# Recurrent mixer of a two-block network: small products ordered over the quarters of the matmul array, two PSUM banks at a time

## The chip, the cores and the metric

The kernel runs on one core of a Trainium2 chip. Its time is the time of one execution on the device, in microseconds (us). TensorE (PE) multiplies matrices into PSUM; VectorE (DVE), ScalarE (ACT) and GpSimd (POOL) do the rest; SyncE (SP) issues most of the transfers.

## The reference, cut to what matters

A sequence of 256 tokens of width 1024 goes through a first block of two layers (a mixer of three branches, then a feed-forward part) and a second block (an attention layer and a state-space layer, with a second, "context", sequence beside). All arithmetic is float32. The change touches one branch of the first block's mixer, the recurrence over tokens, in both directions, of eight heads of 64 channels:

```python
def step(state, inp):
    r_t, w_t, k_t, v_t, kk_t, a_t = inp
    sa = jnp.einsum('bhij,bhj->bhi', state, -kk_t)
    state = (state * w_t[:, :, None, :] + sa[..., None] * (kk_t * a_t)[:, :, None, :]
             + v_t[..., None] * k_t[:, :, None, :])
    return state, jnp.einsum('bhij,bhj->bhi', state, r_t)
...
y = direction(0, False) + direction(1, True)
```

## The kernel before, in words

Large products use weights that are split on the chip into a rounded high part (ACT, line 57) and the rest (DVE or POOL, line 58), and are made of three matmuls each (lines 185 to 187). Weights come from DRAM by SP's queue (line 172) into a ring of four buffers.

The recurrence is turned into small products over four chunks of 64 tokens. `wkv_groups` runs four groups per layer, each of two heads `h`, two directions `d` and four chunks (tile of 128 tokens `t`, half of it `q`), so eight groups in all. A 64-row and 64-column product sits on one quarter of the 128 by 128 array: the half of the partitions of its operands chooses the rows, the half of the partitions of its output the columns. `hs(0)` and `hs(1)` are these halves. A float32 product shows in the trace as two matmul instructions, each with its weight load.

`wkv_group` is a Python generator. It goes beside the large products: each call of `up` (a large product of 24 matmuls) ends with `tick`, which takes the next steps of the generators beside it (2.4 steps per call in layer 0, 1.6 in layer 1, `RATES`). A step is what stands between two `yield`s. The framework then lays out the instructions of each engine in a fixed order: it takes, among those whose inputs are ready in its own model of the times, the one that was emitted first. So a step whose inputs are late is mixed with large products, and on the chip each engine follows the fixed order. What is left of the generator is emitted by `drain("wk")` before the third branch is merged.

The group's steps that the change touches:

- line 585, `ps_l`: matrices between the tokens of a chunk, for `LR` and `AK`. For each head one PSUM bank and one step: eight products, `q` innermost, so two quarters alternate (the rows are those of the head). DVE masks the bank (line 587).
- lines 718, 719 and 721, `ps_n`: what each chunk adds to the state. One bank for each of two halves `b` of the work; three products of one quarter stand together (two only for the first chunk), then those of the other head. Half `b` uses the rows of `q = b`.
- line 735, `ps_c`: the corrections of the states at the chunks' ends, the second (`s = 2`) after the first (`s = 1`), in one step; one small bank for each direction, two products each, read by two instructions of DVE (line 737).
- line 748, `ps_q`: for each `q` a bank with eight products, the columns alternating with the head; DVE adds to it in two instructions (line 750).
- line 769, `ps_y`: the outputs, 30 products of a group in one bank: for each `t` and `q` first one or two with all 128 rows (64 columns, states), then six on the quarter of rows `q` and columns `q`.

All these take turns in three PSUM banks (tag `pa`). Line 691 (`ps_ak`) and line 701 are not touched; they alternate the quarters of rows and columns `q`, within one bank:

```python
for u, (d, h, t) in enumerate(ui):
    for q in range(2):
        mm(pak[hs(q), u], AK8[hs(q), u, 0:64], Vt[hs(q), t, hs(h)], start=True, stop=True)
```

Of the kernel before, what the change touches and what calls it, by code (L numbers as in the profile page):

```python
# [14 lines left out]
P = 128  # L15
# [10 lines left out]
# 2 atanh(z) / z in powers of z^2, |z| <= 1/3  # L26
# [10 lines left out]
# constants of the first block  # L37
# [10 lines left out]
class Weights:  # L48
    """a tile of weights as pairs of rounded high and low parts, made in two pieces."""
# [18 lines left out]
class Core:  # L68
    NR, NH = 4, 5
    dom = "sm"  # L70
    # pairs whose low parts are left to GpSimd, where VectorE has a chain to finish
# [92 lines left out]
    def wsplit(self, src, a, b, rows=False):  # L164
        """a tile [128, a, b] of weights as a pair; src may be two halves, of the last dimension or, with rows, of the partitions."""
# [39 lines left out]
    def fill(self, first=()):  # L205
        """emits work that doesn't depend on x, for the tensor engine to do while the rows of x are normalized; the weights `first` that x meets are loaded before."""
# [17 lines left out]
    def tick(self):  # L224
        """emits the next steps of the work that goes beside."""
# [24 lines left out]
    def drain(self, name=None):  # L250
        """emits the rest of the work beside."""
# [13 lines left out]
    def rsqrt(self, x, n, out=None):  # L265
        """x [128, n] -> x ** -0.5 by Newton's method."""
# [12 lines left out]
    def rsqrt1(self, x):  # L279
        """x [128, 1] -> x ** -0.5 by Newton's method."""  # L280
# [10 lines left out]
    def evac_T(self, src, gcol, bcol, dst, ps=None):  # L291
        """src [128 tok, 2, 128*n] token-major -> dst pair [128, n, 256], channel c scaled and shifted."""
# [13 lines left out]
        for j in range(0, n, 2):  # L306
# [6 lines left out]
            # one engine reads a bank  # L313
# [16 lines left out]
    def ln_rows(self, v, t, rows=None, eps=1e-5):  # L330
        """v[:, t] normalized in place; with rows of scales and shifts, these too."""
# [16 lines left out]
    def layernorm(self, v, gcol, bcol):  # L348
        """v [128 tok, 2, 1024], normalized already; returns the pair of x^T."""
# [9 lines left out]
    def padded(self, tiles):  # L359
        """tiles with zeros in the first and the last column."""  # L360
# [5 lines left out]
    def scaled(self, v, grow, brow, scale):  # L366
        """v [128 tok, 2, 1024], normalized already, becomes scale * x."""
# [7 lines left out]
    def row(self, ap, name="row", q=None):  # L375
        """a vector [n] of DRAM on every partition."""
# [6 lines left out]
class First(Core):  # L383
# [27 lines left out]
    def derived(self, l):  # L411
        """per-channel constants of the layer that are worked out on the chip."""
# [24 lines left out]
    def toeplitz(self):  # L437
        """relb[p, h, c] = rel_bias[bucket(c - p - 128), h], c in 0..383."""
# [17 lines left out]
    def shift(self, l, zt, dst):  # L456
        """project tile zt of the shifted part of w_in and apply the centred token shift; dst [128, 256]."""
# [33 lines left out]
    def wkv_group(self, l, ct):  # L491
        """heads 2 ct and 2 ct + 1, both directions; the result takes the place of r."""
# [84 lines left out]
        for dst, src in ((LR, Bn), (AK, K)):  # L577
            for h in range(2):
                yield
                pl = self.pa([P, 2, 2, P], "ps_l")  # L580
                for d in range(2):
                    for t in range(2):
                        for q in range(2):
                            c = 2 * t + q
                            mm(pl[hs(q), d, t], src[hs(h), d, c * 64:(c + 1) * 64],
                               AR[hs(h), :, d, c * 64:(c + 1) * 64], start=True, stop=True)
                v_.tensor_tensor(dst[:, :, h], pl, self.m_lr.unsqueeze(2).to_broadcast([P, 2, 2, P]), op=ALU.mult)
        # v meets the sum of both directions
# [4 lines left out]
        # blocks of 8 on the diagonal by substitution, each matrix spread over the partitions of its block's rows  # L593
# [23 lines left out]
        # X[:, 1] is the inverse, X[:, 0] its transpose as long as it is of blocks up to 32  # L617
# [26 lines left out]
        # the blocks of 32 off the diagonal, A U B; both directions' share tiles  # L644
# [64 lines left out]
        dcol = lambda d, s: Dt[:, d * 4 + (s if d == 0 else 2 - s):d * 4 + (s if d == 0 else 2 - s) + 1]  # L709
        for b in range(2):  # L710
            pn = self.pa([P, 3, 2, 64], "ps_n")
            for s in range(3):
                d = (s + b) % 2
                c = chunk(d, s)
                t, q = divmod(c, 2)
                for h in range(2):
                    u = d * 4 + h * 2 + t
                    mm(pn[hs(h), s, 0], Bt[hs(q), d, t, hs(h)], WU(hs(q), u, slice(64, 128)), start=True, stop=False)
                    mm(pn[hs(h), s, 0], Kt[hs(q), d, t, hs(h)], Vt[hs(q), t, hs(h)], start=False, stop=True)
                    if s:  # L720
                        mm(pn[hs(h), s, 1], WU(hs(q), u, slice(0, 64)), Bt[hs(q), d, t, hs(h)], start=True, stop=True)
# [9 lines left out]
        for s in (1, 2):  # L731
            for d in range(2):
                pc = self.pa([P, 64], "ps_c")
                for h in range(2):
                    mm(pc[hs(h)], MT[hs(h), d, s - 1], S0[hs(h), d, s - 1, hs(h)], start=True, stop=True)
                for h in range(2):
                    v_.scalar_tensor_tensor(S0[hs(h), d, s, hs(h)], pc[hs(h)], dcol(d, s)[hs(h)], N0[hs(h), d, s - 1],
                                            op0=ALU.mult, op1=ALU.add)
        yield
        Q = self.w1("xx", [P, 2, 2, 2, 64], bufs=self.NX)  # L740
        Rt = AR[:, 1].rearrange("p d (t q i) -> p q d t i", q=2, i=64)
        for q in range(2):
            pq = self.pa([P, 2, 2, 64], "ps_q")
            for d in range(2):
                for t in range(2):
                    for h in range(2):
                        u = d * 4 + h * 2 + t
                        mm(pq[hs(h), d, t], WU(hs(q), u, slice(0, 64)), LR8[hs(q), u, 64:128], start=True, stop=True)
            for d in range(2):
                v_.tensor_tensor(Q[:, q, d], pq[:, d], Rt[:, q, d], op=ALU.add)  # L750

        yield
        py = self.pa([P, 2, P], "ps_y")
        for t in range(2):
            for q in range(2):
                o = py[hs(q), t]
                seq = []
                for d in range(2):
                    c = 2 * t + q
                    s = c if d == 0 else 3 - c  # L760
                    if s:
                        seq.append((o, Q[:, q, d, t], S0[:, d, s - 1]))
                for h in range(2):
                    for d in range(2):
                        u = d * 4 + h * 2 + t
                        seq.append((o[:, hs(h)], LR8[hs(q), u, 64:128], WU(hs(q), u, slice(64, 128))))
                    seq.append((o[:, hs(h)], AK8[hs(q), h * 2 + t, 64:128], Vt[hs(q), t, hs(h)]))
                for i, (oo, a, b) in enumerate(seq):
                    mm(oo, a, b, start=(i == 0), stop=(i == len(seq) - 1), skip_group_check=True)
# [30 lines left out]
    def pool_branch(self, l, j, ya):  # L800
        """groups j and j + 1 of the pooling branch, in two steps."""
# [42 lines left out]
    def down(self, acc, w, k0, nk, x, first, last):  # L844
        """acc[t][h] [128 tok, 512] += x[:, k0..]^T w rows; w [K, 1024] in DRAM, x pair [128, nk, 256]."""
# [109 lines left out]
    def branch(self, l, n, y, m):  # L955
        """m [128, 8, 256] (+)= (1 + tanh(gate / 2)) * (y @ w_branch[n])."""
# [24 lines left out]
    def resid(self, acc, ax, scale, rows=None):  # L981
        """the normalized rows of scale * acc + ax."""
# [8 lines left out]
    def layer(self, l, ax, rows):  # L991
        """ax: the normalized rows, still without the scales and shifts in DRAM."""
# [78 lines left out]
    def start(self):  # L1071
        """x, and what its norm needs, before all else."""
# [25 lines left out]
class Second(Core):  # L1098
    """the second block. The context and the modulation vectors don't depend on x; what they need is emitted beside the first block."""
# [74 lines left out]
    def upto(self, n):  # L1174
        """the same in steps."""
# [4 lines left out]
    def need(self, n):  # L1180
        """emits what is left of the first n parts of the modulation vectors."""
# [3 lines left out]
    def rms(self, x, t):  # L1185
        """[128, 1]: the rows' 1 / sqrt(mean square + eps) of x[:, t]."""
# [10 lines left out]
    def modulate(self, x, l, row, which, dst, *first, inplace=False, ps=None):  # L1197
        """dst pair = the modulated rmsnorm of x, transposed; which 0 for the mixer, 1 for the ffn."""
# [15 lines left out]
    def add_gated(self, x, t, h, g, acc):  # L1214
        """x[:, t, half h] += g * acc."""
# [5 lines left out]
    def down2(self, wtile, kb, pair, res, gate):  # L1221
        """res += gate * (pair^T w); wtile(k, n, h): k tiles k..k+n-1 of w, half h of its columns."""
# [17 lines left out]
    def ffn_ahead(self):  # L1240
        """the first hidden tiles of the context's ffn, to DRAM."""
# [7 lines left out]
    def swiglu1(self, l, j, x):  # L1249
        """the products for hidden tile j of the ffn."""  # L1250
# [715 lines left out]
def _consts():  # L1966
    """arrays that depend on the shapes alone."""
    import numpy as np
    k = {}
# [124 lines left out]
```

## Time and profile before

| | |
|---|---|
| median of 3 runs | 2550.89 us (2545.45 to 2552.18) |
| profiled execution, span from first to last instruction | 2544.6 us |
| TensorE busy | 2403.8 us, 94% |
| VectorE busy | 1810.9 us, 71% |
| ScalarE busy | 1238.4 us, 49% |
| GpSimd busy | 391.8 us, 15% |
| mean traffic of the DMA engines | 159 GB/s |

The profile page gives the profiled execution by its span alone; the runs' times are 0.9 to 7.6 us above it. Busy time is the union of an engine's instructions. Matmuls are pipelined, so the duration of one (0.22 us for a 64 by 64 one) is no cost: the cost is the distance from its start to the start of the next.

### The profile page before, as it was taken

Reading aid. Unit: us, or ns where it says so; the run is one execution under the profiler, and the core shown is the slowest. Engines: PE = TensorE matmul, PEld = TensorE weight load, DVE = VectorE, ACT = ScalarE, POOL = GpSimd, SP = SyncE. Lnnn points to the kernel's source line nnn. Section 1 sums busy time; section 2 is a strip of 40 time slices with the busy share of each in tenths; the row PEclk is TensorE's granted clock in tenths of the full one; section 3 lists DMA queues with packets and bytes.
Section 4 is the critical chain, followed back from the end, with each engine's and each line's share of the span. In section 5 each row is a group of like instructions: output and inputs, shape, how many; then the busy total and the mean of one; then the engine's idle time right before and its main releaser. Section 6 shows DMA issues by size and latency. Waiting matters only on the chain.

```text
span 2544.6 us, 49580 instructions
## 1 busy us (share of the span) xinstructions
PE 2403.8 (94%) x19082; PEld 2104.7 (83%) x19082; DVE 1810.9 (71%) x3997; ACT 1238.4 (49%) x2615; POOL 391.8 (15%) x376
## 2 busy tenths in 40 slices
PE   7999999999998999999999999899899989989998
PEld 5777777788997888778988899778799889987997
DVE  7757866677667858777778666866666689985666
ACT  3334425555553444243455455555555556654554
POOL 4200210122003100200012200300200233231000
PEclk9999999999999999999999999999999989999999
DMA  8744446456666644465556566512466644436664
GB/s 243 234 128 146 139 140 131 141 173 186 184 199 193 186 149 123 124 206 151 166 149 195 171 186 199 131 35 71 145 185 186 174 118 129 125 104 198 209 184 132
DMA packets 513005, 404.94 MB, mean 159 GB/s; under 512 B 49968, under 2 KB 445024, under 8 KB 512000
## 3 DMA queue, kind: packets, MB, share of 16 engines
q1 hardware_dynamic: 511536, 397.41, 52.9%
q0 software_dynamic: 1232, 4.36, 0.5%
q8 instruction: 150, 2.46, 0.4%
q14 instruction: 87, 0.71, 0.1%
HBM read 393.19 MB, written 8.52 MB: 158 GB/s over the span
## 4 chain that ended last, share of the span: by engine, by line
PE 72%; DVE 15%; DMA 4%; ACT 4%; issue 3%; POOL 1%; SPq 0%; ACTq 0%; DVEq 0%; POOLq 0%
PE ps_fg L185 5%; PE ps_fg L186 5%; PE ps_fg L187 4%; PE ps_acc L186 4%; PE ps_acc L187 4%; PE ps_acc L185 4%; DVE wl L58 3%; DMA wr<-in_w_in_dram 2%; PE ps_up L187 2%; PE ps_up L186 2%; PE ps_up L185 2%; PE ps_o L1452 2%; PE acc L185 2%; PE acc L186 2%; PE acc L187 2%
## 5 line engine op out<-in xcount | busy, mean ns | idle before, releaser
L57 ACT CAST wh<-wr 128x512 fp32r<-128x512 f32 (+1 forms) x1212 | 743.7, 622 | 839.7 <-PE ps_fg L186 169.3
L58 DVE TENSOR_TENSOR wl<-wr,wh 128x512 fp32r<-128x512 f32 x1092 | 774.2, 717 | 410.2 <-ACT wh L57 403.3
L58 POOL TENSOR_TENSOR wl<-wr,wh 128x512 fp32r<-128x512 f32 (+1 forms) x120 | 159.8, 1351 | 825.6 <-ACT wh L57 816.6
L186 PE MATMUL ps_fg<-xl,wh 128*128 128x256 f32 x672 | 190.2, 283 | 0.0
L187 PE MATMUL ps_fg<-xh,wl 128*128 128x256 f32 x672 | 190.2, 283 | 0.0
L185 PE MATMUL ps_fg<-xh,wh 128*128 128x256 f32 x672 | 190.1, 283 | 0.0
L186 PE MATMUL ps_acc<-wl,hh 128*128 128x512 f32 x432 | 171.9, 398 | 8.9 <-DVE wl L58 8.9
L185 PE MATMUL ps_acc<-wh,hh 128*128 128x512 f32 x432 | 171.0, 396 | 0.0
L187 PE MATMUL ps_acc<-wh,hl 128*128 128x512 f32 x432 | 170.9, 396 | 0.0
L187 PE MATMUL ps_up<-xh,wl 128*128 128x256 f32 x480 | 135.9, 283 | 0.4 <-POOL wl L58 0.4
L185 PE MATMUL ps_up<-xh,wh 128*128 128x256 f32 x480 | 135.8, 283 | 0.0
L186 PE MATMUL ps_up<-xl,wh 128*128 128x256 f32 x480 | 135.8, 283 | 0.0
L185 PEld LDWEIGHTS ps_fg<-xh,wh 128*128 128x128 f32 x672 | 129.0, 192 | 0.4
L186 PEld LDWEIGHTS ps_fg<-xl,wh 128*128 128x128 f32 x672 | 129.0, 192 | 0.4
L187 PEld LDWEIGHTS ps_fg<-xh,wl 128*128 128x128 f32 x672 | 129.0, 192 | 0.0
L186 PEld LDWEIGHTS ps_acc<-wl,hh 128*128 128x128 f32 x432 | 81.9, 190 | 28.6 <-DVE wl L58 11.1
L185 PE MATMUL ps_fg<-ch,wh 128*128 128x256 f32 x352 | 102.9, 292 | 0.0
L186 PE MATMUL ps_fg<-cl,wh 128*128 128x256 f32 x352 | 101.1, 287 | 0.0
L187 PE MATMUL ps_fg<-ch,wl 128*128 128x256 f32 x352 | 100.3, 285 | 0.8 <-DVE wl L58 0.8
L185 PE MATMUL ps_gl<-xh,wh 128*128 128x256 f32 x336 | 98.8, 294 | 0.1
L187 PEld LDWEIGHTS ps_acc<-wh,hl 128*128 128x128 f32 x432 | 81.9, 190 | 19.1 <-DVE hl L263 0.2
L185 PEld LDWEIGHTS ps_acc<-wh,hh 128*128 128x128 f32 x432 | 81.9, 190 | 18.0 <-ACT hh L262 0.2
(656 smaller groups left out, 6865.7 us busy)
## 6 DMA issues: line engine op xcount, KB each, us to landing
wr<-in_w_in_dram SPq DMA_DIRECT2D x110, 512.0 KB
adw<-in_ada_w_dram SPq DMA_DIRECT2D x96, 512.0 KB
wr<-in_ssm_w_in_dram SPq DMA_DIRECT2D x72, 512.0 KB
wr<-in_ffn_w_gate_dram SPq DMA_DIRECT2D x66, 512.0 KB
wr<-in_ffn_w_up_dram SPq DMA_DIRECT2D x66, 512.0 KB
wr<-in_ffn_w_down_dram SPq DMA_DIRECT2D x66, 512.0 KB
wr<-in_w_up_dram SPq DMA_DIRECT2D x64, 512.0 KB
wr<-in_w_down_dram SPq DMA_DIRECT2D x64, 512.0 KB
```

Of the source, the lines that this page charges most:

```text
L57: nc.scalar.copy(hi, raw[:, i:i + self.n])
L58: z = (nc.gpsimd if core.spare > 0 else nc.vector).tensor_tensor(lo, raw[:, i:i + self.n], hi.bitcast(F32), op=ALU.subtract)
L185: mm(out, ah, bh, start=first, stop=False)
L186: mm(out, ah, bl, start=False, stop=False)
L187: mm(out, al, bh, start=False, stop=last)
L1452: mm(po[HS[e], c, t], kvs[kb // 2][1][:, kb % 2, g * 64:(g + 1) * 64], at[:, kb], start=(kb == 0), stop=(kb == nk - 1))
```

## The change

The same products are computed, with the same operands. Their order and their banks change, and so do the steps. The rest of the diff takes out comments and docstrings.

```diff
         for dst, src in ((LR, Bn), (AK, K)):
-            for h in range(2):
-                yield
-                pl = self.pa([P, 2, 2, P], "ps_l")
-                for d in range(2):
-                    for t in range(2):
+            yield
+            pls = [self.pa([P, 2, 2, P], "ps_l") for _ in range(2)]
+            for d in range(2):
+                for t in range(2):
+                    for h in range(2):
                         for q in range(2):
                             c = 2 * t + q
-                            mm(pl[hs(q), d, t], ...
+                            mm(pls[h][hs(q), d, t], ...
-                v_.tensor_tensor(dst[:, :, h], pl, ...
+            for h in range(2):
+                v_.tensor_tensor(dst[:, :, h], pls[h], ...
+            yield
...
+        pns = [self.pa([P, 3, 2, 64], "ps_n") for _ in range(2)]
+        for s in range(3):
+            for i in range(3 if s else 2):
+                for b in range(2):
+                    pn = pns[b]
+                    d = (s + b) % 2
+                    t, q = divmod(chunk(d, s), 2)
+                    for h in range(2):
+                        (the product i of the three, as before)
         for b in range(2):
-            pn = self.pa([P, 3, 2, 64], "ps_n")
-            (for each s and h: the two or three products)
+            pn = pns[b]
...
-        for s in (1, 2):
-            for d in range(2):
-                pc = self.pa([P, 64], "ps_c")
-                for h in range(2):
-                    mm(pc[hs(h)], MT[hs(h), d, s - 1], S0[hs(h), d, s - 1, hs(h)], start=True, stop=True)
-                (two instructions of DVE)
-        yield
+        def step(s):
+            pc = self.pa([P, 2, 64], "ps_c")
+            for d in range(2):
+                for h in range(2):
+                    mm(pc[hs(h), d], MT[hs(h), d, s - 1], S0[hs(h), d, s - 1, hs(h)], start=True, stop=True)
+            (four instructions of DVE)
+        step(1)
+        yield
+        step(2)
+        yield
...
-        for q in range(2):
-            pq = self.pa([P, 2, 2, 64], "ps_q")
-            for d in range(2):
-                for t in range(2):
+        pqs = [self.pa([P, 2, 2, 64], "ps_q") for _ in range(2)]
+        for d in range(2):
+            for t in range(2):
+                for q in range(2):
                     for h in range(2):
                         u = d * 4 + h * 2 + t
-                        mm(pq[hs(h), d, t], ...
+                        mm(pqs[q][hs(h), d, t], ...
-            for d in range(2):
-                v_.tensor_tensor(Q[:, q, d], pq[:, d], Rt[:, q, d], op=ALU.add)
+        for q in range(2):
+            v_.tensor_tensor(Q[:, q], pqs[q], Rt[:, q], op=ALU.add)
...
         py = self.pa([P, 2, P], "ps_y")
+        seq = [[], []]
...
+        (seq[q]: first the products with states, of both t; then the others, t outermost)
-                for i, (oo, a, b) in enumerate(seq):
-                    mm(oo, a, b, start=(i == 0), stop=(i == len(seq) - 1), skip_group_check=True)
+        for i in range(len(seq[0])):
+            for q in range(2):
+                mm(*seq[q][i], start=(i == 0), stop=(i == len(seq[q]) - 1), skip_group_check=True)
```

A group has one step more than before (the correction's second half is a step of its own); the steps around `ps_l` keep their number. Each half of `seq` has 15 products, three of them with 128 rows.

## Rows read from the trace of the kernel before

**Rows 1.** The page: the chain that ended last, by engine.

```profile
PE 72%; DVE 15%; DMA 4%; ACT 4%; issue 3%; POOL 1%; SPq 0%; ACTq 0%; DVEq 0%; POOLq 0%
```

**Rows 2.** Busy time by stretch: stretch, length, then each engine, clock, DMA.

```profile
100.00:390.00 290.00, 278.29 (x3354) 225.54 (x3353) 216.28 (x672) 109.06 (x248) 47.30 (x61) 0.99 0.49 147
390.00:500.00 110.00, 108.22 (x699) 85.21 (x699) 66.73 (x190) 61.82 (x177) 4.44 (x4) 1.00 0.52 128
500.00:850.00 350.00, 328.28 (x2209) 298.54 (x2208) 243.08 (x403) 173.88 (x311) 71.35 (x51) 0.97 0.63 188
850.00:1235.00 385.00, 372.79 (x3952) 312.75 (x3952) 287.38 (x796) 150.89 (x323) 34.35 (x49) 0.99 0.50 151
```

**Rows 3.** Busy time on ps_y, ps_l, ps_n and ps_c, then L748 by line.

```profile
sum 850.00, PE 42.55 PEld 34.27 DVE 6.77; mean PE 21.27 PEld 17.14 DVE 3.38
...
sum 850.00, PE 28.78 PEld 23.51 DVE 21.48; mean PE 14.39 PEld 11.76 DVE 10.74
...
sum 850.00, PE 20.15 PEld 17.85 DVE 20.13; mean PE 10.07 PEld 8.93 DVE 10.06
...
sum 850.00, PE 12.38 PEld 7.59 DVE 18.13; mean PE 6.19 PEld 3.79 DVE 9.06
...
L748 PE MATMUL ps_q<-w_LR,w_xx 64*64 64x64 f32 x256 | 8.4, 224 | 0.0
```

**Rows 4.** Timeline of PE at a group's outputs: start, us, instruction, count.

```profile
381.41 0.43 PE L769 MATMUL ps_y<-s,w_xx 128*64 128x128 f32 x2 [0.45 <-DVE w_xx L750]
381.77 0.44 PE L769 MATMUL ps_y<-w_xx,w_LR 64*64 64x64 f32 x4
...
382.61 0.65 PE L769 MATMUL ps_y<-s,w_xx 128*64 128x128 f32 x4
383.19 0.44 PE L769 MATMUL ps_y<-w_xx,w_LR 64*64 64x64 f32 x4
```

**Rows 5.** Timeline of PE at L691, and what comes next.

```profile
140.39 1.15 PE L691 MATMUL ps_ak<-w_Vt,w_AK 64*64 64x64 f32 x32
141.47 0.39 PE L187 MATMUL ps_qk<-xh,wl 128*128 128x256 f32 x1
```

**Rows 6.** Timeline of PE at L585: one head, then two heads mixed.

```profile
187.73 1.09 PE L585 MATMUL ps_l<-w_AR,w_Bn 64*64 64x128 f32 x16
188.75 1.13 PE L906 MATMUL ps_lg<-ak,aq 64*128 64x256 f32 x4
...
192.60 0.28 PE L585 MATMUL ps_l<-w_AR,w_Bn 64*64 64x128 f32 x2
192.66 0.28 PE L585 MATMUL ps_l<-w_AR,w_K 64*64 64x128 f32 x2
192.71 0.28 PE L585 MATMUL ps_l<-w_AR,w_Bn 64*64 64x128 f32 x2
```

**Rows 7.** Timeline of PE at ps_n.

```profile
146.83 0.22 PE L718 MATMUL ps_n<-w_xx,w_Bt 64*64 64x64 f32 x1
146.83 0.22 PE L721 MATMUL ps_n<-w_Bt,w_xx 64*64 64x64 f32 x1
146.84 0.22 PE L718 MATMUL ps_n<-w_xx,w_Bt 64*64 64x64 f32 x1
146.88 0.22 PE L719 MATMUL ps_n<-w_Vt,w_Kt 64*64 64x64 f32 x1
```

**Rows 8.** Timeline of PE at the corrections, two groups.

```profile
149.38 0.28 PE L187 MATMUL ps_qk<-xh,wl 128*128 128x256 f32 x1
149.50 0.28 PE L185 MATMUL ps_qk<-xh,wh 128*128 128x256 f32 x1
149.71 0.45 PE L735 MATMUL ps_c<-s,w_MT 64*64 64x64 f32 x8
...
233.89 0.32 PE L735 MATMUL ps_c<-s,w_MT 64*64 64x64 f32 x2
```

**Rows 9.** Timeline of DVE at the corrections.

```profile
150.48 1.23 DVE L737 SCALAR_TENSOR_TENSOR s<-ps_c,Dt,w_N 64x64 f32<-64x64 f32 x4
```

More of the change, by code (lines that the diff above doesn't have):

```diff
@@ L577, in wkv_group @@
         for dst, src in ((LR, Bn), (AK, K)):
-            for h in range(2):
-                yield
-                pl = self.pa([P, 2, 2, P], "ps_l")
-                for d in range(2):
-                    for t in range(2):
+            yield
[3 more added lines that the diff above has]
+                    for h in range(2):
                         for q in range(2):
                             c = 2 * t + q
-                            mm(pl[hs(q), d, t], src[hs(h), d, c * 64:(c + 1) * 64],
+                            mm(pls[h][hs(q), d, t], src[hs(h), d, c * 64:(c + 1) * 64],
                                AR[hs(h), :, d, c * 64:(c + 1) * 64], start=True, stop=True)
-                v_.tensor_tensor(dst[:, :, h], pl, self.m_lr.unsqueeze(2).to_broadcast([P, 2, 2, P]), op=ALU.mult)
+            for h in range(2):
+                v_.tensor_tensor(dst[:, :, h], pls[h], self.m_lr.unsqueeze(2).to_broadcast([P, 2, 2, P]), op=ALU.mult)
+            yield
         g_.tensor_tensor(AK[:, 0, :, :, 64:128], AK[:, 0, :, :, 64:128], AK[:, 1, :, :, 64:128], op=ALU.add)
@@ L709, in wkv_group @@
         dcol = lambda d, s: Dt[:, d * 4 + (s if d == 0 else 2 - s):d * 4 + (s if d == 0 else 2 - s) + 1]
-        for b in range(2):
-            pn = self.pa([P, 3, 2, 64], "ps_n")
[L712 to L715, printed above, removed]
-                for h in range(2):
[L717 to L721, printed above, removed]
+        pns = [self.pa([P, 3, 2, 64], "ps_n") for _ in range(2)]
[6 more added lines that the diff above has]
+                    for h in range(2):
+                        u = d * 4 + h * 2 + t
+                        if i == 0:
+                            mm(pn[hs(h), s, 0], Bt[hs(q), d, t, hs(h)], WU(hs(q), u, slice(64, 128)), start=True, stop=False)
+                        elif i == 1:
+                            mm(pn[hs(h), s, 0], Kt[hs(q), d, t, hs(h)], Vt[hs(q), t, hs(h)], start=False, stop=True)
+                        else:
+                            mm(pn[hs(h), s, 1], WU(hs(q), u, slice(0, 64)), Bt[hs(q), d, t, hs(h)], start=True, stop=True)
+        for b in range(2):
+            pn = pns[b]
             for s in range(3):
@@ L730, in wkv_group @@
         yield
-        for s in (1, 2):
-            for d in range(2):
-                pc = self.pa([P, 64], "ps_c")
-                for h in range(2):
-                    mm(pc[hs(h)], MT[hs(h), d, s - 1], S0[hs(h), d, s - 1, hs(h)], start=True, stop=True)
-                for h in range(2):
-                    v_.scalar_tensor_tensor(S0[hs(h), d, s, hs(h)], pc[hs(h)], dcol(d, s)[hs(h)], N0[hs(h), d, s - 1],
-                                            op0=ALU.mult, op1=ALU.add)
-        yield
         Q = self.w1("xx", [P, 2, 2, 2, 64], bufs=self.NX)
         Rt = AR[:, 1].rearrange("p d (t q i) -> p q d t i", q=2, i=64)
-        for q in range(2):
-            pq = self.pa([P, 2, 2, 64], "ps_q")
+        def step(s):
+            pc = self.pa([P, 2, 64], "ps_c")
             for d in range(2):
-                for t in range(2):
+                for h in range(2):
+                    mm(pc[hs(h), d], MT[hs(h), d, s - 1], S0[hs(h), d, s - 1, hs(h)], start=True, stop=True)
+            for d in range(2):
+                for h in range(2):
+                    v_.scalar_tensor_tensor(S0[hs(h), d, s, hs(h)], pc[hs(h), d], dcol(d, s)[hs(h)], N0[hs(h), d, s - 1],
+                                            op0=ALU.mult, op1=ALU.add)
+        step(1)
[6 more added lines that the diff above has]
+                for q in range(2):
                     for h in range(2):
                         u = d * 4 + h * 2 + t
-                        mm(pq[hs(h), d, t], WU(hs(q), u, slice(0, 64)), LR8[hs(q), u, 64:128], start=True, stop=True)
-            for d in range(2):
-                v_.tensor_tensor(Q[:, q, d], pq[:, d], Rt[:, q, d], op=ALU.add)
+                        mm(pqs[q][hs(h), d, t], WU(hs(q), u, slice(0, 64)), LR8[hs(q), u, 64:128], start=True, stop=True)
+        for q in range(2):
+            v_.tensor_tensor(Q[:, q], pqs[q], Rt[:, q], op=ALU.add)
         yield
         py = self.pa([P, 2, P], "ps_y")
+        seq = [[], []]
         for t in range(2):
             for q in range(2):
-                o = py[hs(q), t]
-                seq = []
                 for d in range(2):
@@ L761, in wkv_group @@
                     if s:
-                        seq.append((o, Q[:, q, d, t], S0[:, d, s - 1]))
-                for h in range(2):
+                        seq[q].append((py[hs(q), t], Q[:, q, d, t], S0[:, d, s - 1]))
+        for t in range(2):
+            for h in range(2):
+                for q in range(2):
+                    o = py[hs(q), t, hs(h)]
                     for d in range(2):
                         u = d * 4 + h * 2 + t
-                        seq.append((o[:, hs(h)], LR8[hs(q), u, 64:128], WU(hs(q), u, slice(64, 128))))
-                    seq.append((o[:, hs(h)], AK8[hs(q), h * 2 + t, 64:128], Vt[hs(q), t, hs(h)]))
-                for i, (oo, a, b) in enumerate(seq):
-                    mm(oo, a, b, start=(i == 0), stop=(i == len(seq) - 1), skip_group_check=True)
+                        seq[q].append((o, LR8[hs(q), u, 64:128], WU(hs(q), u, slice(64, 128))))
+                    seq[q].append((o, AK8[hs(q), h * 2 + t, 64:128], Vt[hs(q), t, hs(h)]))
+        for i in range(len(seq[0])):
+            for q in range(2):
+                mm(*seq[q][i], start=(i == 0), stop=(i == len(seq[q]) - 1), skip_group_check=True)
         yield
```

## Prediction, made before the changed kernel ran

> **What bounds the kernel now.** I read the page first. Its chain of waits runs 72% through TensorE and 15% through VectorE [rows 1], so TensorE's time counts, but not all of it. Then the stretches. The recurrent mixer's small products stand in two: in 100 to 390 us TensorE is busy 278.3 of 290 us, in 850 to 1235 us 372.8 of 385 us, at a granted clock of 0.99 [rows 2], its 2.4 GHz level. TensorE is full there, 96 and 97%; VectorE is at 75% in both (216.3 of 290, 287.4 of 385). After the first, 390 to 500 us is dense too, 108.2 of 110 us [rows 2]: the mixer's chain has ended there and other products go on. So no one waits for the mixer's last step; what is taken from TensorE inside the stretch moves all that follows. Only then the small products themselves, by tile and by timeline.
>
> The reader is to see one thing in the timelines: the cost of a small matmul is the distance between starts, and this depends on its neighbours. In the outputs (`ps_y`) twelve matmuls of one quarter stand between 381.77 and 382.61 us [rows 4]: 0.84 us, 0.07 each with the changes of shape. Where two quarters alternate, 32 of the same shape take 140.39 to 141.47 us [rows 5]: 1.08 us, 0.034 each. So two quarters overlap, and the stretch costs half. In `ps_l` 16 matmuls of 64x128 on two quarters of one head take 187.73 to 188.75 us, 1.02 us for 8 pairs, 0.13 a pair; where the end of one head's work meets the start of the other's, pairs start at 192.60, 192.66 and 192.71 us, 0.055 apart [rows 6]. That is four quarters at once: the second pair of quarters, other rows and another bank, costs nothing. In `ps_n` four matmuls of 64x64 start within 146.83 to 146.88 us [rows 7], so these overlap beyond two as well.
>
> **The change part by part.** The measure is busy time on TensorE over both stretches [rows 3], eight groups.
>
> Outputs, `ps_y`: 42.55 us, 5.3 a group. A group has 12 matmuls with 128 rows and 48 on quarters. Two of the former take 0.36 us with the change of shape (381.41 to 381.77), four 0.58 (382.61 to 383.19) [rows 4]: 0.11 each and 0.14 for the change. Afterwards they stand together and their column halves alternate: 6 pairs by 0.11 and 0.14 once are 0.80 us. The 48 alternate as in rows 5: 1.08 us for 32 and 16 more by 0.03 (0.06 a pair) are 1.56. Together 2.36 against 5.3: 2.9 a group, 23 us. Bounds: if the 128-row halves do not overlap, which no row shows for this shape, 6 x 0.11 x 8 = 5 less, 18; if the quarters do not (48 by 0.058, which is 0.84 less 0.14 over twelve, and 0.22 at the edges, 3.0), 3.8 a group, 12 saved; if neither does, 4.5, and only the fewer changes of shape are left: 6 us. I take 23, since rows 5 are the same shape and the same alternation.
>
> Chunk matrices, `ps_l`: 28.78 us. Afterwards 16 bursts (two per group) of 32 matmuls on four quarters. By rows 6 a burst of eight fours costs what eight pairs cost now, 1.09 us with its tail: 17.4. Saved: 11 us. Bounds: 0 if the second pair is not free, 11 if it is; rows 6 show it, so I take 11.
>
> State parts, `ps_n`: 20.15 us, 2.5 a group. 64 matmuls in 16 fours; at 0.058 a four, the distance of pairs in rows 5, 0.93, and 0.22 at the edges (1.15 less 16 x 0.058 in rows 5), 1.2 us. But the half `b = 1` needs the other direction's copy from ScalarE, so I expect the burst to fall in two, the first on two quarters only: 1.6. Saved: 0.9 a group, 7 us. Bounds: with pairs only 32 by 0.058 and the edges twice, 2.3, saves 2; one full burst 10. I take 7.
>
> Corrections, `ps_c`: 12.38 us. In the first correction eight stand together, 0.45 us; the second falls into bursts of two, 0.32 each [rows 8]. An entry costs also the matmul before it 0.09 (149.50 to 149.71 is 0.21, the usual distance, 149.38 to 149.50, 0.12). Both whole would be 16 x 0.45 = 7.2 and three entries less per group, 2: 7 us saved. The second still waits for each of VectorE's four instructions, so it may stay split and save nothing. I take 4, nearly the middle: in a step of its own more of the four is done by then.
>
> State products, `ps_q`: 8.4 us. 16 pairs by 0.06 become 8 fours, 0.48 less in each group if the fours overlap wholly; with the edges I take 3 us, bounds 0 and 4. VectorE's additions fall from 32 instructions to 16, which is off the path.
>
> One step more per group delays the mixer's end by a call of `up` or two per layer. That is hidden by the dense stretch behind [rows 2]; without it, some 3 us a call. No weight, DMA or issue is moved. VectorE's two masks of a pair of heads now come after both, off the path for the same reason.
>
> Sum: 23 + 11 + 7 + 4 + 3 = 48 us of TensorE; by the lower bounds 6 + 0 + 2 + 0 + 0 = 8, by the upper 23 + 11 + 10 + 7 + 4 = 55. How much arrives? At most the 96 to 97% of a full TensorE, at least the chain's 72%. Weights must come some 7% faster (48 of 675 us): 147 and 151 GB/s become about 160, and 500 to 850 us runs at 188 [rows 2], so the supply holds. I take 80%, nearer to the chain, for its part on VectorE does not shrink: 38 us. The profiled span, 2544.6 us, becomes 2506; it lies 6.3 us under the median, so the time is 2550.9 - 38, 2512 to 2513. I say 2512.
>
> A rule speaks against the largest term. In the outputs the alternating quarters lie in different rows but write one bank. Rows 5 have just that and show 0.034 us each. The Trainium skill, TensorEngine Tiling (Array Packing), section Gotcha 1: PSUM Pressure, says that different row tiles cannot use the same PSUM bank at the same time. By it the outputs would save 12 us, as in the second bound above, and the sum would be 37; by the trace 23 and 48. The trace decides for this shape.
>
> A second one touches the fours of 64 columns. Rows 7 show four starts in 0.05 us. The Trainium skill, TensorE: Matmul & The Clock Gate, section "Wait — 56ns, not 53.3ns?", gives a floor of about 25 ns between starts, by which a four would cost an estimated 0.1 us, `ps_q` would save nothing and `ps_n` 3, and the sum would be 41. The rows show less between starts, so I keep 48.
>
> **The rivals.**
>
> Pairs only (15%). Row halves exclude each other where the order is steady, and rows 6 and 7 show only seams between two pieces of work. Then `ps_l` and `ps_q` save nothing, `ps_n` 2, the corrections 4; the outputs keep 23 if one bank is no obstacle, 12 if it is. 29 or 18 us, by 80% 23 or 14: 2528 to 2537. For it: no long run on four quarters is in the trace. Against: rows 6, three pair starts at half the distance. It is also what the first rule above would bring.
>
> Supply takes half (12%). TensorE gets ahead of the splits of weights: VectorE, 75% busy, does them between the mixer's own instructions, and the wait moves to the large products. Half of 48 arrives: 2527. Against: VectorE has a quarter free.
>
> All of it arrives (13%), since VectorE no longer stands at the front of its queue behind `ps_y` for 5.3 us: 48 to 55 us, 2496 to 2503.
>
> Slower (5%). The three banks: two are taken at once, so TensorE, whose order is fixed, stands where the next pair of banks, or the second correction with all four states in one bank, waits for VectorE; four of its instructions take 1.23 us [rows 9]. If it stood that long at six places of a group (both `ps_l`, `ps_n`, both corrections, `ps_q`), this is 6 x 8 x 1.23 = 59 us against 48: 11 us slower, 2562. It decides from 1.0 us a place on. Behind it are large products, and all engines that wait for them. Against: TensorE now has only 11.7 and 12.2 us free in the two stretches [rows 2], with the same three banks.
>
> That the products do not change place, since the framework reorders them, is the case of no change (5%): it mixes only what is not ready, and within a step all becomes ready together.
>
> **How the numbers follow.** Forecast 50%, its own range 2503 to 2526. Low end 2490: all 55 us and 5 of waits. High end 2540: a little over the worse end of "pairs only"; "slower", "no change" and a little more are left out, about 12%. Over 0.3% is 7.7 us, 2543 and 2559 the marks, about what can be told from no change here. Faster: 50 + 15 + 12 + 13, less 2 for tails: 88%. Same: 5 and these 2, 7%. Slower 5%.
>
> **What would show it.** `ps_y` near 2.4 us a group as one burst, the 128-row matmuls first; `ps_l` as 16 bursts of about 1.1 us; busy time on `ps_l` near 17, `ps_n` 13, `ps_y` 19. Wrong if a burst of four quarters takes twice 1.1 us, if `ps_y` stays at 0.058 a matmul, or if TensorE's free time in the two stretches grows by more than 20 us.

## The result, and the profile after

The changed kernel takes 2512.68 us, the median of four runs (2510.18 to 2514.42), against 2548.17 us of the kernel before beside it: ratio 0.9868, 95% interval 0.9851 to 0.9884, 35.5 us less. The forecast was 2512. In a later round its ratio was 0.9869 (0.9847 to 0.9892).

The page of the profiled run (2511.67 us, span 2509.7): busy time by engine, and further down the chain that ended last, which answers to [rows 1].

```profile
PE 2359.1 (94%) x19082; PEld 2072.0 (83%) x19082; DVE 1811.0 (72%) x3981; ACT 1234.1 (49%) x2615; POOL 388.9 (15%) x376
...
PE 70%; DVE 16%; DMA 5%; issue 4%; ACT 4%; POOL 1%; SPq 0%; DVEq 0%; ACTq 0%; POOLq 0%
```

The first number is the one to read. TensorE runs the same 19082 matmuls in 2359.1 instead of 2403.8 us, 44.7 less. The span fell by 34.9 (2544.6 to 2509.7). So TensorE's free time over the whole span grew by 9.8 us: that is the part of the saving that did not arrive.

Busy time by stretch, as [rows 2] (the stretches end earlier now): stretch, length, then each engine, granted clock, DMA share, GB/s.

```profile
100.00:375.00 275.00, 260.78 (x3324) 213.76 (x3324) 215.51 (x658) 109.34 (x249) 44.77 (x60) 0.98 0.54 160
...
490.00:835.00 345.00, 324.36 (x2174) 294.71 (x2175) 237.62 (x390) 170.53 (x305) 66.33 (x49) 0.97 0.62 189
835.00:1202.00 367.00, 351.61 (x3969) 296.19 (x3968) 285.93 (x777) 150.55 (x321) 34.67 (x49) 0.98 0.54 161
```

The first product with layer 0's output weights starts at 520.6 us, before at 533.4, and the mixer of layer 1 is left 32 us earlier (its last transposes of this phase at 1291.9 and 1324.0): 13 us come from layer 0 and 19 from layer 1. TensorE is free 14.2 and 15.4 us in them, before 11.7 and 12.2: 5.7 of the 9.8 us (17.7 and 16.2 us in a second profile of the same kernel, `after_2`, so this split holds to some 3 us). The supply of weights runs at 160 and 161 GB/s, as forecast.

Busy time on the products, over both stretches, in the order ps_y, ps_l, ps_n, ps_c, and the state products' line, against [rows 3].

```profile
sum 860.00, PE 21.07 PEld 17.63 DVE 6.77; mean PE 10.53 PEld 8.82 DVE 3.39
...
sum 860.00, PE 19.61 PEld 15.50 DVE 20.60; mean PE 9.81 PEld 7.75 DVE 10.30
...
sum 860.00, PE 11.45 PEld 9.68 DVE 20.14; mean PE 5.73 PEld 4.84 DVE 10.07
...
sum 860.00, PE 9.13 PEld 6.17 DVE 18.12; mean PE 4.57 PEld 3.09 DVE 9.06
...
L763 PE MATMUL ps_q<-w_LR,w_xx 64*64 64x64 f32 x256 | 8.5, 225 | 0.0
```

Against before that is 21.5, 9.2, 8.7 and 3.3 us less, and nothing on the state products: 42.6 together. A second profile (`after_2`) has the same four sums within 0.01 us, so they are far steadier than the page's total.

The timeline of PE shows how: start, duration, instruction, count. First a chunk-matrix burst, as [rows 6]; then a part of the state parts, as [rows 7]; then two output groups, as [rows 4]: one torn (cut in two by other work) after its first two matmuls, and one whole.

```profile
187.77 1.10 PE L586 MATMUL ps_l<-w_AR,w_Bn 64*64 64x128 f32 x32
188.80 0.38 PE L185 MATMUL ps_br<-yah,wh 128*128 128x256 f32 x1
...
149.20 0.22 PE L724 MATMUL ps_n<-w_xx,w_Bt 64*64 64x64 f32 x1
149.21 0.22 PE L726 MATMUL ps_n<-w_Vt,w_Kt 64*64 64x64 f32 x1
149.21 0.22 PE L724 MATMUL ps_n<-w_xx,w_Bt 64*64 64x64 f32 x1
149.21 0.22 PE L726 MATMUL ps_n<-w_Vt,w_Kt 64*64 64x64 f32 x1
149.26 0.22 PE L724 MATMUL ps_n<-w_xx,w_Bt 64*64 64x64 f32 x1
...
157.06 0.43 PE L788 MATMUL ps_y<-s,w_xx 128*64 128x128 f32 x2
157.43 0.38 PE L185 MATMUL ps_qk<-xh,wh 128*128 128x256 f32 x1
157.65 0.28 PE L186 MATMUL ps_qk<-xl,wh 128*128 128x256 f32 x1
157.85 0.87 PE L788 MATMUL ps_y<-s,w_xx 128*64 128x128 f32 x10
...
235.88 0.88 PE L788 MATMUL ps_y<-s,w_xx 128*64 128x128 f32 x12
236.69 0.45 PE L788 MATMUL ps_y<-w_xx,w_LR 64*64 64x64 f32 x8
...
238.24 0.49 PE L925 MATMUL ps_lg<-ak,aq 64*128 64x256 f32 x2
```

Read starts, not durations. In `ps_l`, 32 matmuls on four quarters take 187.77 to 188.80 us, 1.03; before, 16 took 1.02. In `ps_n` four start within 0.02 us, and the next four begin 0.06 after the first. In `ps_y` the whole group stands from 235.88 to 238.24, 2.36 us: 12 matmuls with 128 rows in 0.81, the 48 small ones in 1.55. The forecast had 0.80 and 1.56.

### The profile page after: what moved, and what is told of

The parts are those of the page before. It is cut to its first block, busy times and chain, and to the rows that moved or that the text cites. A ratio compares the mean times of both kernels' runs of the same rounds, so it can differ in the third digit from the quotient of the medians.

```text
span 2509.7 us, 49557 instructions
## 1 busy us (share of the span) xinstructions
PE 2359.1 (94%) x19082; PEld 2072.0 (83%) x19082; DVE 1811.0 (72%) x3981; ACT 1234.1 (49%) x2615; POOL 388.9 (15%) x376
## 4 chain that ended last, share of the span: by engine, by line
PE 70%; DVE 16%; DMA 5%; issue 4%; ACT 4%; POOL 1%; SPq 0%; DVEq 0%; ACTq 0%; POOLq 0%
PE ps_fg L185 4%; PE ps_fg L187 4%; PE ps_fg L186 4%; PE ps_acc L186 4%; PE ps_acc L187 4%; PE ps_acc L185 4%; DVE wl L58 3%; DMA wr<-in_w_in_dram 3%; PE ps_up L187 2%; PE ps_up L186 2%; PE ps_up L185 2%; PE ps_o L1471 2%; PE acc L186 2%; PE acc L187 2%; PE acc L185 2%
## 5 line engine op out<-in xcount | busy, mean ns | idle before, releaser
L186 PE MATMUL ps_gl<-xl,wh 128*128 128x256 f32 x336 | 97.9, 291 | 0.0
```

The costliest lines, as they stand in the source:

```text
L186: mm(out, ah, bl, start=False, stop=False)
```

## The experiments

Each was timed against the kernel before on its own chip, so the ratios are compared. 0.001 of ratio is 2.5 us.

**The outputs by themselves, and everything but the outputs.** `y_only` is the kernel before with only the new order of the output products; `y_old` is the changed kernel with the old order. The part that `y_only` puts in, and `y_old` takes out:

```
-        for i, (oo, a, b) in enumerate(seq):     # per tile t and quarter q
-            mm(oo, a, b, start=(i == 0), stop=(i == len(seq) - 1), ...)
+        for i in range(len(seq[0])):             # 128-row products first
+            for q in range(2):
+                mm(*seq[q][i], start=(i == 0), stop=(i == len(seq[q]) - 1), ...)
```

Expected of the first: 

> The kernel before with the outputs' new order alone. Theory (TensorE's time, freed by overlapping quarters, arrives at the end at some 80%): busy time on ps_y falls from 42.6 to about 21 us, 2.35 us a group, and the time by about 18 us, to 2530. Rival (the gain comes from the new layout of steps and banks): ps_y falls, the time moves by less than 8 us. Rival (it all arrives): 21 us, 2527.

Expected of the second: 

> The changed kernel with the outputs' old order. Theory: ps_y back at 42 us busy, 5.24 us a group, the other tiles as in the changed kernel, the time 18 us over the changed one: 2531. If the parts do not add up (they free the same waits), it and the run with the new outputs alone together save clearly more or less than the 35.5 us of the whole change.

Measured: `y_only` 0.9933 (0.9912 to 0.9954), `y_old` 0.9937 (0.9917 to 0.9957). Their gains, 0.0067 and 0.0063, add to 0.0130; the whole change has 0.0132. So the parts add up within the intervals: 17 us by the outputs and 16 by the four others together. The sums on `ps_y`, of `y_only` and `y_old`:

```profile
sum 860.00, PE 22.17 PEld 18.44 DVE 6.76; mean PE 11.09 PEld 9.22 DVE 3.38
...
sum 860.00, PE 42.48 PEld 34.27 DVE 6.77; mean PE 21.24 PEld 17.14 DVE 3.38
```

Against the kernels without and with the new order, 42.55 and 21.07, that is 20.4 and 21.4 us of busy time. They became 17 and 18 us of time, a little over four fifths. The four other terms give 21.1 us busy and 16 to 17 of time, about the same share within the intervals. The state parts and the corrections have no experiment of their own: what they gave in time is not shown one by one.

**Fewer changes of shape, or overlapping quarters?** The order of the outputs does two things: all 128-row products stand together, and the quarters alternate. `y_grouped` keeps the first alone.

```
-        for i in range(len(seq[0])):
+        for part in (range(3), range(3, len(seq[0]))):
             for q in range(2):
-                mm(*seq[q][i], ...)
+                for i in part:
+                    mm(*seq[q][i], ...)
```

Expected: 

> The changed kernel; in the outputs the 128-row products still stand first, but the two quarters one after the other and not in turn. Theory (overlap of quarters): 4.5 us a group in place of 2.35, ps_y near 36 us busy, the time 12 to 14 us over the changed kernel: 2525. Rival (the fewer changes of shape make the saving): 2.4 to 3 us a group, at most 4 us over: 2516.

Measured: 0.9914 (0.9894 to 0.9934), 0.0046 or 11.7 us above the changed kernel's ratio. The two intervals just do not meet (0.9884 and 0.9894), so the size is rough. One group's timeline of PE, and the sum on `ps_y`:

```profile
157.50 1.14 PE L789 MATMUL ps_y<-s,w_xx 128*64 128x128 f32 x12
158.57 0.44 PE L789 MATMUL ps_y<-w_xx,w_LR 64*64 64x64 f32 x4
...
161.34 0.39 PE L185 MATMUL ps_qk<-xh,wh 128*128 128x256 f32 x1
...
sum 860.00, PE 31.22 PEld 28.76 DVE 6.77; mean PE 15.61 PEld 14.38 DVE 3.39
```

A group takes 3.84 us (157.50 to 161.34): the small products of one quarter start 0.058 apart (158.57 to 161.34, 2.77 us for 48), twice the alternating distance. So about half of the 2.9 us that a group saved is the overlap (3.84 to 2.36), and by the time more than half: 11.7 of 17 us. The rest is the grouping: fewer changes of shape, and 128-row halves that overlap in part. No run tells these two apart. The expected 4.5 us a group was too much: it had 1.46 us for the 128-row products and 3.0 for the small ones, and they took 1.07 and 2.77. At the seams, where one half's products end and the other's begin, they overlapped even in this order.

**The second pair of quarters.** `l_pairs` lets the head be the outer loop of the chunk matrices again, in the same banks and the same step.

```
-            for d in range(2):
-                for t in range(2):
-                    for h in range(2):
+            for h in range(2):
+                for d in range(2):
+                    for t in range(2):
```

Expected: 

> The changed kernel; in the chunk matrices both banks and one step stay, but the head is outermost again, so two quarters alternate and four only at the seam. Theory (the third and fourth quarter are free): a burst of 32 takes about 1.6 to 1.9 us in place of 1.03, ps_l busy 28 in place of 19.6, the time 7 to 12 us over the changed kernel: 2520 to 2524. Rival (one step for both heads, and fewer bursts, made the saving): within 3 us of the changed kernel.

Measured: 0.9894 (0.9871 to 0.9916), 0.0026 or 6.6 us above the changed kernel. The intervals overlap, so the time alone does not settle it; the timeline of PE and the sum on `ps_l` do.

```profile
185.43 1.59 PE L586 MATMUL ps_l<-w_AR,w_Bn 64*64 64x128 f32 x32
...
sum 860.00, PE 25.63 PEld 21.73 DVE 20.88; mean PE 12.81 PEld 10.86 DVE 10.44
```

The same 32 matmuls take 1.59 us with their tail in this order and 1.10 in turns, 1.52 and 1.03 to the next start of another product: 6.0 us of busy time over both stretches. So two thirds of the 9.2 us of the chunk matrices are the steady use of all four quarters; the other third came with the longer bursts, which overlap in their middle in this order too. "Pairs only" is out: 32 matmuls on four quarters take 1.03 us, as 16 on two did [rows 6]. Part of the 6.6 us is elsewhere: `ps_y` and `ps_n` were 0.9 and 1.1 us dearer in this run.

**The step between the corrections.** `one_step` takes the added `yield` away:

```
         step(1)
-        yield
         step(2)
```

Expected: 

> After, without the additional step between the first correction and the second (one yield less per group, so that nothing of the other work is placed between them). Theory (the step costs nothing, since a dense stretch follows the mixer, and it gives VectorE time to finish the four states, so that the second corrections stand together more often): time 0 to 6 us over after, corrections 9.1 us busy or more, TensorE waits at the second corrections in more of the groups. Rival (the additional step delays the mixer's chain by about 3 us a call of up, eight of them): time 6 us or more under after.

Measured: 0.9882 (0.9863 to 0.9901), 0.0014 or 3.5 us over the changed kernel, within the scatter. So the added step costs nothing that can be seen, and not the 6 us or more of the rival. But the run changed more than the step: without it all eight output groups are torn after two matmuls, and busy time rises to 23.1 us on `ps_y` (from 21.1), 12.8 on `ps_n` (from 11.5) and 9.6 on `ps_c` (from 9.1). What the delay of a step costs by itself is therefore not shown. TensorE waits at the corrections' line for 0.8 us; in two profiles of the changed kernel it waits for 0.2 and 0.4.

**Where the state products' gain went.** In the changed kernel the timeline of PE shows, after the first corrections at 152.71 us:

```profile
152.71 0.45 PE L747 MATMUL ps_c<-s,w_MT 64*64 64x64 f32 x8
...
154.32 0.28 PE L747 MATMUL ps_c<-s,w_MT 64*64 64x64 f32 x2
154.34 0.27 PE L763 MATMUL ps_q<-w_LR,w_xx 64*64 64x64 f32 x1
154.43 0.23 PE L747 MATMUL ps_c<-s,w_MT 64*64 64x64 f32 x2
154.45 0.60 PE L763 MATMUL ps_q<-w_LR,w_xx 64*64 64x64 f32 x11
...
154.95 0.68 PE L763 MATMUL ps_q<-w_LR,w_xx 64*64 64x64 f32 x19
155.56 0.38 PE L186 MATMUL ps_qk<-xl,wh 128*128 128x256 f32 x1
...
1094.05 0.69 PE L763 MATMUL ps_q<-w_LR,w_xx 64*64 64x64 f32 x32
```

VectorE releases the second corrections two at a time, and they fall in between the state products: 154.32 to 155.56, 1.24 us for both. In five of the eight groups the state products are torn like this. A group that is left alone (1094.05) has its 32 state products in 0.69 us with the tail, 0.63 to the next start. `q_between` moves the state products, which need no corrected state, between the two corrections, with as many steps:

```
         step(1)
         yield
-        step(2)
-        yield
         pqs = [...]; ...          # the state products
+        yield
+        step(2)
```

Expected: 

> After, with the state products (ps_q) moved between the first and the second correction, as many steps as before. In after five of eight groups have the state products torn apart by the second corrections, which VectorE releases one at a time (0.09 + 0.39 + 0.05 + 0.61 us against 0.62 in one burst). Theory (the predicted 3 us of the state products are lost to that mixing, not to a floor of the starts): the state products are eight bursts of 0.62 us, 5.0 us busy against 8.5, the corrections stay near 9, time 2 to 4 us under after (0.1 to 0.15%). Rival (a burst of four quarters of 64 columns has a floor between its starts): a burst stays at 0.9 to 1.1 us and busy time within 1 us of 8.5. If the second corrections then stand alone and split, up to 3 us of it come back on them, and the time is that of after.

Measured: 0.9839 (0.9821 to 0.9857), 2503.75 us. The same place of the timeline of PE, and the three lines:

```profile
154.09 0.38 PE L747 MATMUL ps_c<-s,w_MT 64*64 64x64 f32 x5
...
154.37 0.64 PE L761 MATMUL ps_q<-w_LR,w_xx 64*64 64x64 f32 x30
...
155.82 0.45 PE L747 MATMUL ps_c<-s,w_MT 64*64 64x64 f32 x8
156.20 0.39 PE L186 MATMUL ps_qk<-xl,wh 128*128 128x256 f32 x1
...
L747 PE MATMUL ps_c<-s,w_MT 64*64 64x64 f32 x128 | 7.1, 229 | 0.4 <-DVE w_MT L738 0.2
L787 PE MATMUL ps_y<-s,w_xx 128*64 128x128 f32 x96 | 7.0, 281 | 0.0
L761 PE MATMUL ps_q<-w_LR,w_xx 64*64 64x64 f32 x256 | 6.7, 223 | 0.0
```

The second corrections now stand as eight in 0.38 us: the likely reason is that VectorE had the state products' time to finish the first states. The theory held in its mechanism. Its sizes did not: the state products lost 1.8 us instead of 3.5 (in most groups their first matmuls mix with the last of the first corrections, as at 154.09, and in one they fall into three pieces); the corrections lost 2.0, where I expected none; and the outputs' 128-row products lost 1.7, since no group is torn after two matmuls any more. That is 5.5 us on three lines. The time fell by 0.0029 or 7 us, more than the 2 to 4 expected.

**Products of 32x32 tiles.** `alt32` adds the same idea to two products that the change had left in pairs:

```
-        for d in range(2):
-            for u in range(4):
+        for u in range(4):
+            for d in range(2):
                 for q in range(2):
```

Expected: 

> After, with one thing more: the products of 32x32 tiles (lines 654 and 661, 7.0 and 4.8 us busy in the profile of after) get their direction d inside u, so that four tiles alternate instead of two. Theory (what counts is how many tiles alternate, at any size): they halve, 4 to 6 us less busy on these two lines, time 3 to 5 us under after, 0.1 to 0.2% (ratio to before about 0.985). Rival (tiles of 32 columns start already as fast as they can with two, the cost is what is around them): busy time of the two lines within 1 us of after, time within 2 us of after.

Measured: 0.9864 (0.9841 to 0.9888), no gain beside 0.9868. The two lines are 1.5 and 1.2 us less busy, 2.7 together, and neither theory's number came: the timeline of PE has 32 of them in 0.45 us with the tail (0.39 to the next start), where the changed kernel needs 0.60 (0.53). First `alt32`, then the changed kernel:

```profile
297.25 0.45 PE L661 MATMUL ps_x<-w_xx,w_iu 32*32 32x32 f32 x32
...
297.06 0.60 PE L661 MATMUL ps_x<-w_xx,w_iu 32*32 32x32 f32 x32
```

The steady distance fell by half (fours start 0.032 apart, before pairs did), but the burst ends in 0.12 us that do not shrink, and in the changed kernel the seam between its two directions already overlapped. The page's total for TensorE did not fall (2360.2 against 2359.1 us). One reason can be read from this profile: from 999 to 1002 us the granted clock was 0.50, the 1.2 GHz level, with TensorE busy before and in it (in the changed kernel it was 1.00 there), and the outputs, corrections and state products of the group around it were 1.2 us dearer than in the changed kernel.

**Both, and all beside each other.** `q_between_alt32` has both edits:

Expected: 

> After, with both: the state products between the corrections and the 32x32 products alternating over four tiles. Theory (the savings of TensorE's busy time add, and four fifths arrive): 6 to 9 us less busy than after, time 5 to 8 us under it, 0.2 to 0.3% (ratio to before about 0.984). Rival (TensorE is already waiting for VectorE where these stand): busy time falls as much but the time stays within 2 us of after.

Measured: 0.9832 (0.9810 to 0.9854), 2499.26 us: 0.0036 or 9 us under the changed kernel, a little more than expected, and 0.0007 under `q_between`. As the gains lay near the scatter, three kernels ran once more on one chip.

Expected of the changed kernel: 

> After itself, as the measure for the two beside it on the same chip: ratio to before 0.985 to 0.989, as before in other rounds. If it were below 0.985, what the other order of the state products gave would be the chip's own scatter.

Expected with the state products moved: 

> The state products between the corrections, beside after on the same chip. Theory (their move takes 5.5 us from TensorE's busy time, 1.8 on the state products, 2.0 on the corrections, 1.7 on the outputs, and gives back some waiting): 5 to 9 us under after, 0.2 to 0.35%. Rival (what the first rounds showed beyond the busy time was scatter between rounds): 3 us or less under after.

Expected with both: 

> Both additions, beside after on the same chip. Theory (busy time: 5.5 and 2.7 us less, four fifths and more arrive): 7 to 13 us under after, 0.3 to 0.5%, and 2 to 3 us under the kernel with the state products alone. Rival (the 32x32 products are worth nothing, as alone): the same time as with the state products alone within 1 us.

Measured: 0.9869 (0.9847 to 0.9892), 0.9831 (0.9809 to 0.9853) and 0.9834 (0.9811 to 0.9857); medians 2509.94, 2502.75 and 2502.49 us. The state products' move is worth 0.3 to 0.4%, 7 to 10 us, in both rounds. In each round the two intervals still overlap by 0.0006; that the rounds agree, and that the three lines are the same in both profiles, makes the gain likely and its size rough. The 32x32 edit on top is worth nothing that can be seen, so its expected 2 to 3 us did not come. The page's totals for TensorE in this round, of the changed kernel:

```profile
PE 2353.6 (94%) x19082; PEld 2065.6 (82%) x19082; DVE 1809.7 (72%) x3981; ACT 1233.4 (49%) x2615; POOL 390.2 (16%) x376
```

and with the state products moved:

```profile
PE 2344.2 (94%) x19082; PEld 2060.1 (83%) x19082; DVE 1812.2 (73%) x3981; ACT 1233.3 (49%) x2615; POOL 388.2 (16%) x376
```

Their spans are 2505.1 and 2495.3 us: 9.8 less, of which 9.4 is busy time; TensorE's free time is the same, 151.5 and 151.1. The three lines explain 5.5 of it; some is on the matmuls around, which a torn burst makes dearer (in the changed kernel's timeline above, 157.43 to 157.65 is 0.22 us to the next start, where [rows 8] have 0.12 undisturbed). How much of the rest is that was not measured. A caution stands here too: one kernel's total differed by 5.5 us between two profiles (2359.1 and 2353.6; the mean granted clock was 0.975 in the first and 0.980 in the second), so a single profile's total settles no smaller question.

## Why the prediction was right

**The bound.** TensorE full in the two stretches, nobody waiting for the mixer's last step: right. The additional step cost nothing that `one_step` could show, and time followed TensorE's busy time on these products in every experiment that changed it by 5 us or more.

**Outputs, 23 us.** 21.5 came. A whole group takes 2.36 us as forecast, the column halves of the 128-row products overlapping too (0.07 us a matmul instead of 0.11), which no row had shown. Four of the eight groups are torn after two matmuls, at 0.36 us each (157.06 to 157.43), 1.4 us. The Trainium skill, TensorEngine Tiling (Array Packing), section Gotcha 1: PSUM Pressure, says that different row tiles cannot use the same PSUM bank at the same time. For quarters that differ in rows and in output partitions the trace disagrees: both `ps_y` quarters write one bank, and 48 of their matmuls take 1.55 us in turns, 2.77 one quarter after the other. The prediction also says that this rule would bring "pairs only". It would not: in the chunk matrices, the state parts and the state products, quarters of other rows have a bank of their own.

**Chunk matrices, 11 us.** 9.2 came. The bursts are what [rows 6] promised, 1.03 us. Eight bursts by 1.10 us would be 8.8 us in each layer; the first has 10.07, the second 9.54. In the second layer one burst is torn after ten matmuls (948.01) and one takes 1.39 us (1032.45); why was not traced. In the first the rest is at two places where both bursts of a group stand together, as the timeline of PE shows (the first row is of the one, the others of the other):

```profile
260.77 1.09 PE L586 MATMUL ps_l<-w_AR,w_K 64*64 64x128 f32 x22 [0.44 <-DVE w_LR L589]
...
335.67 1.10 PE L586 MATMUL ps_l<-w_AR,w_Bn 64*64 64x128 f32 x32
336.59 0.81 PE L586 MATMUL ps_l<-w_AR,w_K 64*64 64x128 f32 x10
338.67 1.09 PE L586 MATMUL ps_l<-w_AR,w_K 64*64 64x128 f32 x22 [1.26 <-DVE w_LR L589]
```

and that of VectorE:

```profile
336.12 1.90 DVE L58 TENSOR_TENSOR wl<-wr,wh 128x512 fp32r<-128x512 f32 x2
337.94 1.28 DVE L589 TENSOR_TENSOR w_LR<-ps_l,c_c 128x512 f32<-128x512 f32 x2
```

The second burst wants the banks of the first, whose masks (L589) stand on VectorE behind two weight splits, 1.90 us. This is the mechanism of the rival "slower", at two places and 1.26 us at the longest; it had wanted 1.0 us at six places of every group.

**State parts, 7 us.** 8.7 came. In five groups the burst falls in two, 8 in 0.38 and 56 in 1.08 us, as forecast in kind; in three of the second layer it does not fall, 64 in 1.09.

**Corrections, 4 us.** 3.3 came, by a choice in the middle of wide bounds, which is luck more than reasoning: the first correction stands whole, the second is split in six of the eight groups, before in all. `q_between` shows that it can be whole in all.

**State products, 3 us.** Nothing: the failed term. I took a fours' burst alone and did not look at what stands next to it: the second corrections, which I myself expected to stay split, fall into it. The burst by itself is right, 0.63 us. The Trainium skill, TensorE: Matmul & The Clock Gate, section "Wait — 56ns, not 53.3ns?", gives a floor of about 25 ns between starts, which would have brought the same zero for another reason. The trace does not show it between quarters: four start within 0.02 us, and fours follow at 0.058 us.

**What arrives, 80% of 48.** 42.6 us on the products, 35.5 of time, 83%. The two errors, 5 us too much in the sum and 3 points too little in the share, partly cancel: 38 us were forecast. That the time itself, 2512.68 us, meets the forecast 2512 to a microsecond is luck: the 2.5 us that are missing in the saving are made up by the kernel before, whose median fell from 2550.89 to 2548.17 us with a fourth run. The lost part is free time of TensorE, 9.8 us over the span, of which 1.7 stands at the chunk matrices' masks and 5.7 in the two stretches altogether. Another 1.4 is lost ahead of the changed products: the first chunk matrix starts at 106.3 us, before at 104.9. TensorE's list of waits (line, who was waited for, us in total, times, longest) has two more that grew:

```profile
PE ps_z L187 <- DVE wl L58: 6.6, 2, 6.4
...
PE ps_b L606 <- DVE w_xx L603: 5.4, 4, 3.2
```

Before, they were 3.5 us (2.1 at the longest) and 3.3 (1.3). The first, at 39.7 us, is a large product that waits for VectorE's weight split, the mechanism of "supply takes half"; but it stands ahead of the mixer's small products, and other waits shrank (at `ps_b` L530 from 11.1 to 7.8 us), so the 9.8 us have no single cause that is shown. "Supply takes half" is out by the share, "all arrives" by the 9.8 us.

## What to carry to other kernels

Price small matmuls by the distance of starts in a run of the same neighbours, and put products of different array quarters in turn, in the innermost loop: here that halved the distance, even where two quarters write one bank. Then look at what may fall between them: a burst that waits for another engine piece by piece spoils the one behind it, and a product that needs none of those pieces, put ahead, gives the other engine the time. Here, on an engine that was 96 to 97% busy, about four fifths of the gain arrived.

## What the runs showed of the hardware that was not expected

- Column halves of 128-row products overlap as quarters do: 12 matmuls in 0.81 us in turns, 1.07 with each half by itself.
- With the quarters one after the other in the program, the end of one's products and the start of the other's overlap by themselves (32 chunk matmuls in 1.52 us with one head after the other, not twice 1.02). In `l_pairs` the second head starts when three pairs of the first are still to start; in `y_grouped` the second quarter starts when three matmuls of the first are still to start, among the 128-row ones (157.78 us) as among the small ones (159.80 us). So starts do not follow the order in which the kernel emits the products. Whether TensorE lets them pass or the framework had reordered them is not shown, since the trace does not hold the program's order.
- Four tiles of 32x32 start within 0.02 us and the next four 0.032 after the first; a burst pays about 0.09 us at its end beyond the usual distance, at three sizes (32 columns: 0.12 us from the last start to the next, less 0.032; 64: 0.15 less 0.058; 128: 0.20 less 0.11).
